# A new opening for a hybrid encoder block: 512-column value products first, conditioning rows on VectorE

## The chip, the core and the metric

The kernel runs on one NeuronCore of a Trainium2 chip. The metric is device time in microseconds (us) of one execution. In this text TensorE is PE in the profile (PEld is its weight load), VectorE is DVE, ScalarE is ACT, GpSimd is POOL, and SP is the SyncE queue that issues nearly all DMAs.

## The reference

One encoder block on a sequence of 1024 positions with 1024 features, in float32:

```
ada = silu(c) @ w_ada + b_ada            # six vectors of 1024: shift1 scale1 gate1 shift2 scale2 gate2
h = rmsnorm(x, g_mix) * (1 + scale1) + shift1
qa,ka,va,qb,kb,vb,ga,gb = split(h @ w_in)          # 6 x 512 and 2 x 1024 columns
oa = mixture_of_dilations(qa, ka, va, rel_bias)     # branch A: three banded patterns, 8 heads
ob = neighbourhood_attention_2d(qb, kb, vb, rpb)    # branch B: 2-D window, 8 heads
merged = sigmoid(ga) * (oa @ w_branch_dil) + sigmoid(gb) * (ob @ w_branch_na)
x = x + gate1 * (merged @ w_out)
h2 = rmsnorm(x, g_ffn) * (1 + scale2) + shift2
u = depthwise_conv3(h2 @ w_up)                      # 5632 columns
x = x + gate2 * ((gelu(u_gate) * u_val) @ w_down)
out = rmsnorm(x, g_final)
```

Only the opening matters here: the vector `ada`, the first norm, h, and the first products out of `w_in`.

## The kernel before, in words

**Products.** Features lie on the 128 partitions, in 8 tiles (k = 0 to 7); positions lie along the free dimension in two halves of 512. A float32 product is made of three products of rounded parts: each operand is split into a high part (`hi`, a copy in the type float32r) and a low part (`lo`, the rest), and TensorE adds hi x hi, hi x lo and lo x hi in PSUM (lines 77 to 79, and 247 to 249 for the value products). A split is one ScalarE copy (L55) and one subtraction on GpSimd or VectorE (L56).

**Conditioning.** `w_ada` comes in 12 chunks of 512 columns (2 MB each, four DMAs of two rows). VectorE multiplies each of the 8 row tiles by silu(c), one number a partition, and adds them up (`ada_rows`, L155 the first row, L157 the others); for the first four chunks ScalarE and GpSimd take some of the rows (`ada_rows_pool`, L161 and L163) and L166 joins the two sums. Four one-column matmuls with a vector of ones then add over the partitions (`ada_sums`, L141), and a VectorE op adds the bias (`piece_bias`, L263 and L265; L148 for the later chunks). The first four chunks are cut so that chunk q holds shift and scale of the feature tiles 2q and 2q + 1: h's tiles can be made two by two as the pieces come.

**h.** For a half, ScalarE squares x (L186), VectorE adds the squares (L188), TensorE adds over partitions (L91), a short chain makes 1/rms (L96 to L98), and four transposes spread it over the partitions (`pbc`, L104). x is multiplied by that (`scale_x`, L206: some tiles on VectorE, most on GpSimd); then ScalarE makes the high part of h (L212), VectorE makes h once more (L214) and subtracts (L215).

**Order.** The opening of the first half, and the norm of the second, are written out by hand for all five engines (`manual_schedule`, L288). Behind each piece of `ada` stand two feature tiles of h, their matmuls for the first q and k tiles (two products of 512 columns) and for four blocks of 128 positions of the first 256 value columns (hv = 0). Behind the hand-written part a planner with a simulated timeline orders the work: the second half of q and k, the rest of the values (256 columns at a time, st counts blocks of 128 positions, `v_product`), the copies of the values to DRAM and their rearrangement there (`va_chunks`, `vb_chunks`), the chunks 4 to 11 of `ada`, then eight rounds of attention (four of branch A, four of branch B) with the q/k products of the next round and the gate products between them. The pools of the opening are released ahead of attention, and attention's tiles (biases, values, softmax) lie where they were.

## Time and profile before

| | |
|---|---|
| runs shown | 1593.29, 1603.09, 1605.68 us (median 1603.09) |
| the profiled execution | 1599.1 us, span 1597.3 us, mean granted TensorE clock 0.98 |
| TensorE busy | 1504.6 us, 94% of the span |
| VectorE, ScalarE, GpSimd busy | 68%, 51%, 48% |
| first product of the opening starts | 27.71 us |
| attention runs on from | 199.23 us |

A timeline row reads: start, length, engine, source line, operation, the tile written and the tile read, shapes, how many were merged, and in brackets the idle time of the engine ahead of it and what ended it. Matmul lengths overlap, so the step from one to the next is read from their starts. In the busy tenths of the page each digit is one fortieth of the span, about 40 us.

### The profile page before, as it was taken

How to read it: one execution, taken by the hardware profiler on the slowest of the kernel's cores; microseconds unless marked ns; L12 is line 12 of the kernel's file. 1: busy time of each engine (PE TensorE's matmuls, PEld its weight loads, DVE VectorE, ACT ScalarE, POOL GpSimd, SP SyncE). 2: the span in 40 equal slices, each digit the busy share in tenths (PEclk: the TensorE clock that was granted, in tenths of full speed). 3: DMA queues.
4: the chain of work that ended last, by engine and by line, in shares of the span. 5: the costliest groups of instructions: out<-in, count | busy, mean ns of one | idle time of the engine just before them, and what ended most of it. 6: DMA issues, size and time to landing. Idle time of an engine off the chain costs nothing. (4 is left out here: it accounts for less than half of the span.)

```text
span 1597.3 us, 21951 instructions
## 1 busy us (share of the span) xinstructions
PE 1504.6 (94%) x7884; PEld 1283.0 (80%) x7884; DVE 1078.5 (68%) x1905; ACT 819.2 (51%) x1479; POOL 769.8 (48%) x490
## 2 busy tenths in 40 slices
PE   4898899999999999999989889999999999999998
PEld 3898888888988888888768777788888887778787
DVE  6886476666767666535542799876666667786765
ACT  4531175666766677544344544344444446475542
POOL 4452133332324444411136767676666665678621
PEclk9898999999999999999999999999999999999999
DMA  6749922222223434446544312222222223533313
GB/s 231 262 137 319 281 61 85 68 89 72 79 80 112 131 108 115 156 133 210 173 144 159 112 53 80 80 92 92 80 79 80 79 80 138 161 129 120 112 53 106
DMA packets 113525, 196.87 MB, mean 123 GB/s; under 512 B 40328, under 2 KB 61704, under 8 KB 113416
## 3 DMA queue, kind: packets, MB, share of 16 engines
q1 hardware_dynamic: 113144, 195.20, 37.3%
q8 instruction: 62, 1.02, 0.3%
q14 instruction: 47, 0.39, 0.1%
q10 hardware_dynamic: 272, 0.26, 0.1%
HBM read 158.73 MB, written 42.47 MB: 126 GB/s over the span
## 5 line engine op out<-in xcount | busy, mean ns | idle before, releaser
L56 POOL TENSOR_TENSOR wlo<-wraw,whi 128x1024 fp32r<-128x1024 f32 (+2 forms) x77 | 177.6, 2306 | 299.1 <-ACT whi L55 285.5
L77 PE MATMUL pj<-h,whi 128*128 128x512 f32 x448 | 182.2, 408 | 17.5 <-DVE kl L429 9.8
L78 PE MATMUL pj<-h,whi 128*128 128x512 f32 x448 | 180.5, 403 | 1.2 <-DVE h L215 1.2
L79 PE MATMUL pj<-h,wlo 128*128 128x512 f32 x448 | 180.4, 403 | 0.0
L56 POOL TENSOR_TENSOR wsl<-big,wsh 128x1024 fp32r<-128x1024 f32 (+1 forms) x45 | 108.9, 2422 | 49.4 <-ACT wsh L55 49.4
L1061 DVE SCALAR_TENSOR_TENSOR big<-wc,sm,big 128x256 f32<-128x256 f32 (+1 forms) x132 | 118.9, 948 | 17.3 <-ACT big L1055 17.2
L55 ACT ACTIVATE whi<-wraw 128x1024 fp32r<-128x1024 f32 (+2 forms) x81 | 81.0, 1000 | 68.9 <-PE pj L78 35.8
L77 PEld LDWEIGHTS pj<-h,whi 128*128 128x128 f32 x448 | 85.7, 192 | 35.4 <-issue 7.0
L78 PEld LDWEIGHTS pj<-h,whi 128*128 128x128 f32 x448 | 86.3, 193 | 16.9 <-DVE h L215 2.3
L79 PEld LDWEIGHTS pj<-h,wlo 128*128 128x128 f32 x448 | 86.1, 192 | 15.5
L542 ACT ACTIVATE P<-P,st 128x256 f32<-128x256 f32 x128 | 64.2, 503 | 47.7 <-DVE st L541 47.3
L541 DVE CUSTOM_DVE_ANT_0 P<-S,bias 128x256 f32<-128x256 f32 x128 | 52.2, 421 | 47.8 <-PE S L588 36.3
L474 POOL TENSOR_TENSOR vv<-vv 96x256 fp32r<-96x256 f32 (+2 forms) x32 | 40.9, 1289 | 84.3 <-ACT vv L473 53.6
L157 DVE SCALAR_TENSOR_TENSOR wada<-wada,cs 128x512 f32<-128x512 f32 x67 | 65.7, 980 | 20.4 <-DMA wada<-w_ada 18.5
L694 POOL TENSOR_SCALAR P<-P,stb 128x288 f32<-128x288 f32 (+1 forms) x32 | 40.1, 1254 | 81.4 <-DVE stb L691 63.6
L1061 DVE SCALAR_TENSOR_TENSOR big<-pj,sm,big 128x512 f32<-128x512 f32 x132 | 67.8, 563 | 16.4 <-ACT big L1055 16.4
L429 DVE SCALAR_TENSOR_TENSOR kl<-pj,ks 64x512 fp32r<-64x512 f32 x64 | 56.3, 880 | 30.6 <-ACT ks L427 30.0
L1055 ACT ACTIVATE big<-wc,sm 128x512 f32<-128x512 f32 x44 | 35.8, 815 | 76.6 <-DVE wc L878 46.1
L247 PE MATMUL pv<-vwh,h 128*128 128x256 f32 x256 | 74.0, 289 | 0.0
L249 PE MATMUL pv<-vwh,h 128*128 128x256 f32 x256 | 73.5, 287 | 0.0
L248 PE MATMUL pv<-vwl,h 128*128 128x256 f32 x256 | 73.0, 286 | 0.0
L56 POOL TENSOR_TENSOR wsl<-wraw,wsh 128x768 fp32r<-128x768 f32 (+1 forms) x23 | 49.9, 2168 | 43.3 <-ACT wsh L55 43.3
(361 smaller groups left out, 4908.6 us busy)
## 6 DMA issues: line engine op xcount, KB each, us to landing
wada<-w_ada SPq DMA_DIRECT2D x47, 512.0 KB, 5.0
wraw<-w_in SPq DMA_DIRECT2D x36, 512.0 KB, 3.8
big<-w_up SPq DMA_DIRECT2D x22, 512.0 KB, 5.5
wraw<-w_up SPq DMA_DIRECT2D x22, 512.0 KB, 3.6
as<-big SPq DMA_DIRECT2D x22, 512.0 KB, 3.0
big<-as SPq DMA_DIRECT2D x22, 512.0 KB, 6.9
wraw<-w_down SPq DMA_DIRECT2D x24, 384.0 KB, 4.1
gs<-gs SPq DMA_DIRECT2D x32, 256.0 KB, 2.0
```

The lines of the kernel that those rows point to most:

```text
L55: act.activation(hi, raw, AF.Copy)
L56: lo_eng.tensor_tensor(lo, raw, f(hi), OP.subtract)
L77: pe.matmul(psum, whi[:, k0 + k], mhi, start=k == 0, stop=False)
L78: pe.matmul(psum, whi[:, k0 + k], mlo, start=False, stop=False)
L79: pe.matmul(psum, wlo[:, k0 + k], mhi, start=False, stop=k == n - 1)
L157: dve.scalar_tensor_tensor(acc, wt[t], cs[:, t:t + 1], acc, OP.mult, OP.add)
L247: pe.matmul(p, hhi, hi[:, k], start=fresh and k == 0, stop=False, skip_group_check=True)
L248: pe.matmul(p, hhi, lo[:, k], start=False, stop=False, skip_group_check=True)
L249: pe.matmul(p, hlo, hi[:, k], start=False, stop=k == KT - 1, skip_group_check=True)
L429: dve.scalar_tensor_tensor(ll[x], pp[a], 0.125, f(kh[a]), OP.mult, OP.subtract)
L542: act.activation(pp, pp, AF.Exp, bias=mi, scale=-1.0, accum_out=li)
L1061: dve.scalar_tensor_tensor(y[:, dst], src, wt, y[:, dst], OP.mult, OP.add)
```

## The change

- **Values first.** The opening makes value products alone, 512 columns wide: the value weights come as a new input `w_v` in four loads of 512 KB a branch, and a 128 x 512 PSUM bank holds one block of 128 positions. The hand-written part now holds all four groups (branch A and B, each half): the first phase makes branch A's first half, two feature tiles behind each piece; then come B first half, A second half, B second half as 24 steps of 12 matmuls. The first q and k products come behind all that, all four of them, and the chunks 4 to 11 of `ada` stand between the steps: VectorE's rows at every second step from 4 to 18, their sums at every second step from 9 to 23. The weights for q and k are split at step 12, and `va_chunks` is issued once, at step 17.
- **Rows on VectorE.** ScalarE and GpSimd take no rows of `w_ada`. For the pieces 1 to 3 VectorE takes six rows, and TensorE adds the last two directly (`ada_sums` with silu(c) in place of ones). Whole chunks have tiles of their own.
- **Low parts a tile behind.** x is not scaled on its own any more: VectorE multiplies x by the scale and by 1/rms in one op into PSUM (`stage`), ScalarE makes the high part from it, and VectorE the low part from it, one tile later. GpSimd does only the low parts of the value weights.
- **Idle products.** `warm(n)` issues n products of the identity with itself, whose result nobody reads: 12 ahead of the norm's sums, 3 ahead of the spread of 1/rms, 8 behind it, 6 behind the first piece's sum.
- **Layout.** x comes in four loads of 512 KB a half, the input rearranged on the host for that; the place that loads x again later in the kernel follows the new layout. The pool of the q/k tiles and its PSUM banks are allocated behind the opening.

The core of the diff (`-` before, `+` after):

```diff
-    def modulate(x, hf, ks, lo_eng):
-        for k in ks:
-            a, b = am1[:, k:k + 1], ada[:, k:k + 1]
-            hi, lo = h[hf, k] = h_tile(), h_tile()
-            act.activation(hi, x[k], AF.Identity, bias=b, scale=a)
-            t = early.tile([128, 512], FT, name="mt", bufs=4)
-            dve.tensor_scalar(t, x[k], a, b, OP.mult, OP.add)
-            lo_eng[k % 2].tensor_tensor(lo, t, f(hi), OP.subtract)
+    def modulate(x, hf, ks, pb):
+        last = ()
+        for k in [*ks, None]:
+            if k is not None:
+                hi, lo = h[hf, k] = h_tile(), h_tile()
+                t, b = stage(), ada[:, k:k + 1]
+                dve.scalar_tensor_tensor(t, x[k], am1[:, k:k + 1], pb, OP.mult, OP.mult)
+                act.activation(hi, t, AF.Identity, bias=b)
+            if last:
+                dve.scalar_tensor_tensor(*last, OP.add, OP.subtract)
+            last = k is not None and (lo, t, b, f(hi))
+    def warm(n):
+        for _ in range(n):
+            pe.matmul(idle, idt, idt, start=True, stop=True)
+    def v_split(raw, w, kp):
+        for i in range(2):
+            split(raw[:, i], w[0][:, 2 * kp + i], w[1][:, 2 * kp + i], pool)
+    def v_products(w, hf, k, banks, ts=range(4)):
+        hi, lo = w
+        for t in ts:
+            p = banks[t]
+            hhi, hlo = (x[:, t * 128:t * 128 + 128] for x in h[hf, k])
+            pe.matmul(p, hhi, hi[:, k], start=k == 0, stop=False, skip_group_check=True)
+            pe.matmul(p, hhi, lo[:, k], start=False, stop=False, skip_group_check=True)
+            pe.matmul(p, hlo, hi[:, k], start=False, stop=k == KT - 1, skip_group_check=True)
...
+        idle = ps.tile([128, 512], FT, name="pj", bufs=5)[:, :128]
+        warm(12)
+        accs = squares(x[0], (dve, dve))
+        pcol = norm_sums(accs)
+        acc = ada_rows(rows[0], range(3))
+        r = rstd_of(pcol, 4)
+        warm(3)
+        pb = bcast(r, ps, "pc")
+        acc = ada_rows(rows[0], range(3, 8), acc)
+        warm(8)
+        v_split(raws[0], vw[0], 0)
+        pa = ada_sums([(acc, ones)])
+        warm(6)
+        banks = v_banks()
+        for q in range(4):
+            piece_bias(q, pa)
+            modulate(x[0], 0, range(2 * q, 2 * q + 2), pb)
+            v_products(vw[0], 0, 2 * q, banks)
             if q < 3:
+                v_split(raws[q + 1], vw[0], q + 1)
+                acc = ada_rows(rows[q + 1], range(6))
+                pa = ada_sums([(rows[q + 1][t], cs[:, t:t + 1]) for t in (6, 7)], stop=False)
             else:
+                accs = squares(x[1], (dve, dve))
+            v_products(vw[0], 0, 2 * q + 1, banks, (0, 1))
+            if q < 3:
+                ada_sums([(acc, ones)], pa)
+            v_products(vw[0], 0, 2 * q + 1, banks, (2, 3))
+        raws = [v_load(1, kp) for kp in range(4)]
+        vw.append((t16("b1"), t16("b2")))
+        rows = {4: ada_load(4, "t0"), 5: ada_load(5, None)}
+        pcol = norm_sums(accs)
+        r = rstd_of(pcol, 4)
+        for kp in range(2):
+            v_split(raws[kp], vw[1], kp)
...
+        for n in range(24):
+            g, k = divmod(n, 8)
+            br, hf = ((1, 0), (0, 1), (1, 1))[g]
+            if k == 0:
+                v_out(*old)
+                banks = v_banks()
+                old = br, hf, banks
+            if n == 17:
+                va_chunks(slice(0, 512))
+            v_products(vw[br], hf, k, banks)
+            if n == 0:
+                pb = bcast(r, ps, "pc")
+                for kp in (2, 3):
+                    v_split(raws[kp], vw[1], kp)
+                modulate(x[1], 1, range(8), pb)
+            if n in (5, 6):
+                qk_raw.append(w_load(w_in[4 * (n - 5)]))
+            i = n // 2 - 2
+            if n % 2 == 0 and 0 <= i < 8:
+                accs[i] = ada_rows(rows[4 + i], range(KT))
+                if i < 6:
+                    rows[6 + i] = ada_load(6 + i, (None, "t0")[i % 2 == 0])
+            if n % 2 and n >= 9:
+                i = (n - 9) // 2
+                ada_bias(4 * (i + 4), ada_sums([(accs[i], ones)]))
+            if n == 12:
+                qk_w = [w_split(qk_raw[i], pool) for i in range(2)]
+        v_out(*old)
...
-    qk = qk_tiles(0, 0, qk_w, qk_psum)
...
+    qk = qk_tiles(0, 0, qk_w)
...
-        "xT": x[0][_POS].T.reshape(KT, 128, S),
+        "xT": x[0][_POS].T.reshape(4, 2, 128, 2, 512).transpose(3, 0, 2, 1, 4),
```

More of the change, by code (lines that the diff above doesn't have):

```diff
@@ L217, in v_load @@
[L217 to L231 removed]
+    xpool = tc.alloc_tile_pool(name="xs", bufs=4, side="right", reuse_waits="tile")
@@ new lines, in hybrid_encoder, with t16, small_tile, stage @@
+    early = tc.alloc_tile_pool(name="early", bufs=1, reuse_waits="tile")
+    ps = tc.alloc_tile_pool(name="ps0", bufs=1, space=PSUM, reuse_waits="tile")
+    def t16(tag, dtype=FR):
+        return tpool.tile([128, KT, 512], dtype, name=tag)
+    def small_tile():
+        return early.tile([128, 512], FT, name="mt", bufs=6)
+    def stage():
+        return ps.tile([128, 512], FT, name="st", bufs=2)
+    def ada_sums(parts, pa=None, stop=True):
+        first = pa is None
+        pa = stage() if first else pa
+        for i, (w, col) in enumerate(parts):
+            for m in range(4):
+                pe.matmul(pa[:, m:m + 1], w[:, m * 128:(m + 1) * 128], col, start=first and i + m == 0,
+                          stop=stop and i == len(parts) - 1 and m == 3, skip_group_check=True)
+        return pa
@@ new lines, in ada_rows, with ada_load @@
+    def ada_rows(rows, ts, acc=None):
+        for t in ts:
+            if acc is None:
+                acc = small_tile()
+                dve.tensor_scalar(acc, rows[t], cs[:, t:t + 1], None, OP.mult)
+            else:
+                dve.scalar_tensor_tensor(acc, rows[t], cs[:, t:t + 1], acc, OP.mult, OP.add)
+        return acc
+    def ada_load(j, tag):
+        if tag:
+            tile = t16(tag, FT)
+            tiles = [tile[:, t:t + 2] for t in range(0, KT, 2)]
+        else:
+            tiles = [x_tile().rearrange("p (a b) -> p a b", a=2) for _ in range(4)]
+        for i, t in enumerate(tiles):
+            sp.dma_start(t, w_ada[j][:, 2 * i:2 * i + 2])
+        return [t[:, i] for t in tiles for i in range(2)]
@@ new lines, in ada_bias, with x_load, squares @@
+    def ada_bias(c0, pa):
+        cc = slice(c0, c0 + 4)
+        dve.tensor_tensor(ada[:, cc], pa[:, :4], b_ada[:, cc], OP.add)
+    def x_load(hf):
+        x = []
+        for kp in range(4):
+            t = x_tile() if hf == 0 else wpool.tile([128, S], FT, name=("whi", "wlo")[kp % 2])
+            sp.dma_start(t.rearrange("p (a b) -> p a b", a=2), xT[hf, kp])
+            x += [t[:, 512 * i:512 * i + 512] for i in range(2)]
+        return x
+    def squares(x, engines):
+        accs = []
+        for k in range(KT):
+            sq = small_tile()
+            act.activation(sq, x[k], AF.Square)
+            if k % 4:
+                engines[k // 4].tensor_tensor(accs[-1], accs[-1], sq, OP.add)
+            else:
+                accs.append(sq)
+        return accs
@@ L372, in qk_tiles @@
+        v_out(*old)
+    dve.scalar_tensor_tensor(am2, ada[:, 32:40], 1.0, g_ffn, OP.add, OP.mult)
+    ps.release()
+    early.release()
+    tpool.release()
+    xpool.release()
+    qkpool = tc.alloc_tile_pool(name="qk", bufs=3, reuse_waits="tile")
+    ps_g = tc.alloc_tile_pool(name="psg", bufs=2, space=PSUM, reuse_waits="tile")
+    def qk_tiles(br, pr, ws=None):
         qt, kt = ((0, 4), (12, 16))[br]
```

282 lines of the change are left out of this document (53 added, 229 removed).

## The prediction

> **What bounds the kernel now.** I read the page first, then the busy time by stage, then TensorE's timeline up to the first attention.
>
> ```profile
> span 1597.3 us, 21951 instructions
> PE 1504.6 (94%) x7884; PEld 1283.0 (80%) x7884; DVE 1078.5 (68%) x1905; ACT 819.2 (51%) x1479; POOL 769.8 (48%) x490
> PE   4898899999999999999989889999999999999998
> ```
> ```profile
> 0.00:27.70 27.70, 8.58 (x36) 7.84 (x36) 16.15 (x23) 13.60 (x22) 9.31 (x10) 1.00 0.85 306
> 52.70:64.90 12.20, 9.06 (x41) 7.61 (x42) 8.52 (x13) 3.41 (x5) 2.50 (x2) 0.72 1.01 378
> 75.20:124.40 49.20, 49.09 (x369) 46.66 (x368) 40.02 (x51) 17.69 (x32) 23.07 (x18) 1.00 0.44 145
> 131.60:199.20 67.60, 62.83 (x465) 60.48 (x465) 37.27 (x53) 11.57 (x22) 11.06 (x6) 0.95 0.92 297
> 199.20:400.00 200.80, 199.22 (x1157) 173.53 (x1158) 133.10 (x397) 136.05 (x330) 67.44 (x48) 0.98 0.25 75
> ```
>
> The columns of the second fence are stage, length, busy PE, PEld, DVE, ACT and POOL, granted clock, DMA share, GB/s. TensorE bounds the kernel (94%). Behind 199.2 us, where attention starts, it is busy 199.22 of 200.8 us, so time that the opening saves should reach the end almost whole. The opening's loss sits ahead of 75 us.
>
> ```profile
> 13.18 1.87 PE L91 MATMUL pcol<-ones,sq 128*128 128x1 f32 x8 [0.93 <-DVE sq L188]
> 15.76 1.12 PE L104 MATMUL pbc<-idt,rs 128*128 128x128 f32 x4 [0.70 <-DVE rs L98]
> 27.71 0.80 PE L77 MATMUL pj<-h,whi 128*128 128x512 f32 x1 [3.83 <-ACT h L212]
> ...
> 54.91 0.57 PE L77 MATMUL pj<-h,whi 128*128 128x512 f32 x1 [2.83 <-ACT h L212]
> 56.41 0.79 PE L78 MATMUL pj<-h,whi 128*128 128x512 f32 x1 [0.93 <-DVE h L215]
> 57.01 0.63 PE L79 MATMUL pj<-h,wlo 128*128 128x512 f32 x1
> ...
> 60.84 0.63 PE L79 MATMUL pj<-h,wlo 128*128 128x512 f32 x1
> ...
> 69.57 0.28 PE L247 MATMUL pv<-vwh,h 128*128 128x256 f32 x1
> ...
> 75.15 0.28 PE L249 MATMUL pv<-vwh,h 128*128 128x256 f32 x1
> ...
> 103.19 0.95 PE L141 MATMUL pada<-ones,wada 128*128 128x1 f32 x8
> 104.00 0.36 PE L249 MATMUL pv<-vwh,h 128*128 128x256 f32 x1
> ...
> 131.56 1.84 PE L141 MATMUL pada<-ones,wada 128*128 128x1 f32 x8 [7.19 <-issue]
> 143.91 0.95 PE L141 MATMUL pada<-ones,wada 128*128 128x1 f32 x8
> ...
> 182.35 0.39 PE L77 MATMUL pj<-h,whi 128*128 128x512 f32 x1
> ...
> 192.44 0.40 PE L79 MATMUL pj<-h,wlo 128*128 128x512 f32 x1
> 192.67 0.95 PE L141 MATMUL pada<-ones,wada 128*128 128x1 f32 x8
> 199.23 0.58 PE L557 MATMUL S<-ks,qs 128*128 128x256 f32 x1 [4.80 <-DVE st L541]
> ```
>
> From starts: 48 matmuls of 256 columns lie between 69.57 and 75.15, 0.119 us each; 45 of 512 columns between 182.35 and 192.44, 0.229 us each; after the gap of 54.91, 10 of them between 57.01 and 60.84, 0.426 us each: half rate. One vector sum (L141, "x8") takes 0.81 us (103.19 to 104.00).
>
> **The change, part by part. Matmuls.** Before: 768 value matmuls x 0.119 = 91.4 us. After: 2 branches x 2 halves x 4 tiles x 8 k x 3 = 384 x 0.229 = 87.9: 3.5 us less. The four q/k products (96 x 0.229 = 22 us) only move behind the opening. In the first phase equal work is done: before 96 value matmuls of 256 (11.4 us) and 48 q/k matmuls (11.0), ended at 75.3; after 96 value matmuls of 512 (22.0). I call that end A.
>
> **Up to the first product.** The rows for VectorE, GpSimd, ScalarE and DMA:
>
> ```profile
> 10.85 2.28 DVE L188 TENSOR_TENSOR sq<-sq,mt 128x512 f32<-128x512 f32 x3 [0.51 <-ACT mt L186]
> 16.11 4.19 DVE L157 SCALAR_TENSOR_TENSOR wada<-wada,cs 128x512 f32<-128x512 f32 x3
> ...
> 40.42 0.16 DVE L263 TENSOR_TENSOR ada<-pada,sm 128x4 f32<-128x4 f32 x1 [1.98 <-PE pada L141]
> 52.74 0.15 DVE L263 TENSOR_TENSOR ada<-pada,sm 128x4 f32<-128x4 f32 x1
> 64.93 0.17 DVE L263 TENSOR_TENSOR ada<-pada,sm 128x4 f32<-128x4 f32 x1 [3.17 <-PE pada L141]
> 81.15 2.48 DVE L206 TENSOR_TENSOR h<-h,pbc 128x512 f32<-128x512 f32 x4 [1.62 <-ACT mt L201]
> ```
> ```profile
> L155 DVE TENSOR_SCALAR wada<-wada,cs x12: 456/484/2533, 15.6 to 178.6; 128x512 f32<-128x512 f32 x12
> ...
> L157 DVE SCALAR_TENSOR_TENSOR wada<-wada,cs x67: 743/752/2870, 16.1 to 187.4; 128x512 f32<-128x512 f32 x67
> ```
> ```profile
> 16.79 1.28 POOL L163 TENSOR_TENSOR kl<-kl 128x512 f32<-128x512 f32 x1 [16.37 <-ACT kl L161]
> 43.47 1.49 POOL L56 TENSOR_TENSOR wlo<-wraw,whi 128x512 fp32r<-128x512 f32 x1 [2.56 <-ACT whi L55]
> 81.20 4.04 POOL L206 TENSOR_TENSOR h<-h,mt 128x512 f32<-128x512 f32 x3 [2.50 <-ACT mt L201]
> ```
> ```profile
> 41.03 1.52 ACT L212 ACTIVATE h<-h,ada,am 128x512 fp32r<-128x512 f32 x2 [8.38 <-DVE am L265]
> ```
> ```profile
> GB/s 0 75 290 239 239 335 339 413 401 426 393 371 412 418 401 259 98 350 265 0 0 0 19 287 44 0 177 335 288 254 393 289 25 68 352 376 231 392 430 391
> wada<-w_ada SPq DMA_DIRECT2D x47, 512.0 KB, 5.0
> ```
>
> The second fence is the two groups of row steps: duration min/median/max in ns. A row step (L157) takes 0.75 us, the multiply that opens a chunk (L155) 0.5; beside GpSimd (16.11 against 16.79) it took 1.40. L206, which has one operand in PSUM, took 0.62 beside GpSimd (81.15 against 81.20). The new modulate ops read one operand from PSUM and write PSUM or SBUF. No row writes PSUM from VectorE; I bound such an op by 0.62 and 1.40 and take 0.65, from L206, the nearest.
>
> Squares end at 13.1 (10.85 + 2.28). The new 512 KB loads of x may bring them forward: in slices of 1.5 us the rate is 240 to 290 GB/s while x comes in 256 KB pieces and about 400 with w_ada's 512 KB pieces; I take 1 us. From 12.1: the multiply and two row steps 2.0, rstd 0.7 (the gap of 15.76), five row steps 3.75, twice 0.65 more beside the split on GpSimd: 19.9; the sum, cold like 13.18's, 1.9: the first piece's bias op starts at **22**. Bias and scale 0.6 (40.42 to 41.03), one modulate op 0.65 and one ScalarE op 0.76 (41.03) bring the first product to 24, against 27.71. Of the 29 idle products the last six stand between the sum and the first product: 2.2 us of room, six 128-column products like 15.76's four (0.28 each) 1.7, so nothing; double that if each takes two passes, 1.2 late.
>
> **The loop over pieces.** Before, the bias ops started at 40.42, 52.74 and 64.93: 12.2 us a piece. After, from a bias op: bias 0.6, one modulate op and ScalarE's tile 1.4, and the low part, queued behind the second modulate op, 0.65: 2.7. Then TensorE: 12 matmuls 2.75, rows 6 and 7 as sums 1.6, six matmuls 1.4, the sum 0.8, semaphore 0.2: 9.4. VectorE meanwhile: bias 0.6, four ops 2.6 and a wait 0.3, the multiply 0.5, five row steps 3.75 and up to 2 x 0.65 beside GpSimd: 9.0, then sum and semaphore: 10.0. I take 9.5, and 11 for the first, which starts at half rate (eight matmuls x 0.2 = 1.6). Pieces: 22, 33, 42.5, 52. DMA covers it: x, four pieces of w_ada and the value weights are 12.1 MB, 30 us at 400 GB/s and some 34 with the start, and all but the last piece have tiles of their own (it waits for the first one's, free at 20). A is then 52 + 2.7 + 24 x 0.229 = **60**, against 75.3: **15 us**.
>
> **From A to attention.** Before: 199.2 - 75.3 = 123.9 us with 672 value matmuls 80.0, 48 q/k 11.0, 48 of the next q 11.0, eight sums 6.5, norm 2.4 = 110.9; lost 13.0, of which 7.19 and 4.80 are the two gaps. After: 288 x 0.229 = 66.0, q/k 22.0, next q 11.0, sums 6.5, norm 2.4 = 107.9. New losses: the second half's norm stands ahead of the splits on ScalarE, so branch 1's first weights are split only after TensorE's sums, rstd 0.7, a split at most 0.76 (as L212) and a low part 1.28 to 1.49 (16.79, 43.47): TensorE waits about 2.5 behind its norm sums, and another 1 until the value banks, whose copies (0.76 at most) stand behind those splits, are out. At the end the q product waits for the last copies: 0.5. The attention gap I leave at 2, between 0 (bias and values load while q and k are made) and the 4.80 of now. Sum 6. Gain 13.0 - 6 + 3.0 = **10 us**. The remaining edits (x layout, later q/k pool, reload of x) move no bytes of the rest; I cost them at nothing, covered by a TensorE that is busy 99% there; uncovered, one 0.5 us issue.
>
> VectorE's row steps for the eight later chunks are 0.5 + 7 x 0.75 = 5.8 us a chunk, against 2 x 12 x 0.229 + 0.8 = 6.3 on TensorE: hidden, if data come.
>
> **Sum:** 15 + 10 = 25; for planning behind the opening I take 1 off: **24 us**. The profiled execution took 1599.1 us (span 1597.3 and 1.8 around it); the runs shown are 1593.3 to 1605.7, median 1603.1. From the middle of the profiled time and the median, 1601: **1577 us**.
>
> **The clock rule.** The trace has half rate after an idle stretch of 2.83 and 0.93 us. In my loop the wait between the last matmuls of one piece and the next low part is 0.2 + 2.7 - 1.4 = 1.5 us, so I run it at full rate; were it twice that, the rows would have it at half rate, 24 x 0.2 = 4.8 us a piece. The Trainium skill, "TensorE: Matmul & The Clock Gate", Part 1, says the clock falls after a window of about 3.4 us without work and rises after as long a busy one; by it a wait of 3 us would leave the forecast as it is, where the row of 54.91 makes it 1591.
>
> **Rivals.** *Cold loop* (0.12): gaps add up (a modulate op at 1.40, a late w_ada piece) and TensorE runs at 0.72 as in 52.7 to 64.9: three pieces x 4.8 = 14 us, gain 10, 1591. For it: it does so today. Against: less work on GpSimd, no op in front of modulate.
>
> *Slower: sums in a fixed order* (0.08): the eight later sums now stand in TensorE's written order between value products. Today a chunk takes (192.67 - 143.91) / 4 = 12.2 us, as VectorE waits for w_ada. Counted from the last piece (52), step 0 ends at 16 (A, 8.4; norm, splits and copies, 5; a step, 2.75), and the eighth chunk's sum is due before step 23's end, 22 x 2.75 + 7 x 0.8 later: 82. VectorE starts the chunks at 16 + 8 x 1.5 of modulating = 28, so the eighth is ready at 28 + 8c: delay 8c - 54. It eats the gain from c = 9.8; at 12.2 it is 43.6: 1601 - 24 + 44 = 1621. Behind a late load stand, on SP's queue, the value results on their way out, whose tiles the row steps share. For it: 5.0 us to landing, and a reload that starts only when the tile is read. Against: two whole chunks of tiles instead of one, and no gathers on SP's queue until step 17.
>
> *Attention starts no earlier* (0.10): the planner puts all 4.80 and a cold stretch behind q/k, and shuffles later fillers; 8 to 12 lost: gain 12 to 16, 1587. Nothing in the trace shows the new order, so I cannot exclude it.
>
> *The idle products do nothing* (inside the forecast): they end before the work does, at 1.6 us: 1579.
>
> **Numbers.** Forecast (gain 16 to 34, 1567 to 1585) 0.64: the bounds are A at 56 to 65 (modulate ops and row steps at 0.62 or 1.40, first product late or not) and losses of 4 to 10 behind it. More than that 0.06; the rivals 0.30. About 16 us, 1%, is what a measurement can tell from no change. Faster: 0.64 + 0.06 = 0.70; within: 0.12 + 0.10 = 0.22; slower 0.08. The range leaves out the slower rival and half of the largest gains, and holds the 4 us between profiled time and median: 1560 to 1597.
>
> **What would show it.** First product near 24; pieces at 33, 42.5, 52 by the bias op; matmul starts 0.229 apart through the loop; A at 60; second-half value products gap of 2 to 3; later sums without idle ahead of them; first attention product running from about 172. Wrong if pieces stay 12 apart, if sums wait for DMA, or if the gain to 199 is missing from the span.

## The result, and the profile after

| | before | changed |
|---|---|---|
| median (range), 9 runs each | 1598.93 us (1593.29 to 1605.68) | 1591.39 us (1585.06 to 1596.18) |
| profiled execution, its span | 1599.1, 1597.3 us | 1590.6, 1588.7 us |
| ratio, 95% interval | | 0.9947, 0.9928 to 0.9966 |

The change gains 7.5 us, half of one per cent. The forecast was 1577 us, a gain of 24, with 1560 to 1597 as its range: the time lies in the range, the gain is a third of the one forecast.

The page of the changed kernel, its head:

```profile
span 1588.7 us, 21184 instructions
PE 1513.5 (95%) x7582; PEld 1273.0 (80%) x7582; DVE 1058.9 (67%) x1905; ACT 804.8 (51%) x1451; POOL 741.8 (47%) x475
```

Busy time by stage in the changed kernel; the columns are as in the prediction's second fence:

```profile
22.50:61.10 38.60, 35.17 (x168) 27.53 (x169) 33.17 (x44) 12.05 (x21) 8.14 (x6) 0.91 0.82 316
61.10:70.10 9.00, 7.13 (x32) 5.40 (x31) 0.34 (x2) 6.30 (x13) 6.10 (x5) 0.81 0.62 245
70.10:132.00 61.90, 61.90 (x300) 52.10 (x299) 50.34 (x70) 12.41 (x18) 9.58 (x6) 1.00 0.67 235
132.00:148.20 16.20, 11.45 (x45) 9.27 (x44) 11.31 (x20) 2.33 (x4) 0.00 (x0) 0.79 0.87 352
...
390.00:446.00 56.00, 49.87 (x304) 44.73 (x303) 40.69 (x110) 38.65 (x85) 12.92 (x9) 0.91 0.23 66
```

The second phase runs without a gap (61.90 of 61.90 us), and two stages stand out: 132 to 148 us, where 16.2 us hold 11.45 us of TensorE at a clock of 0.79, and 390 to 446 us, far behind the opening, with 49.87 of 56 us at 0.91.

TensorE's timeline in the opening of the changed kernel (start, length, idle ahead and what ended it):

```profile
22.52 0.50 PE L236 MATMUL pj<-a,h 128*128 128x512 f32 x1 [0.52 <-ACT h L202]
...
30.30 1.05 PE L140 MATMUL st<-ones,mt 128*128 128x1 f32 x8 [1.24 <-DVE mt L151]
...
40.98 1.05 PE L140 MATMUL st<-ones,mt 128*128 128x1 f32 x8 [0.34 <-DVE mt L151]
...
51.67 1.05 PE L140 MATMUL st<-ones,mt 128*128 128x1 f32 x8 [1.13 <-DVE mt L151]
...
63.98 0.49 PE L236 MATMUL pj<-b,h 128*128 128x512 f32 x1 [1.01 <-ACT b L55]
...
137.78 1.47 PE L140 MATMUL st<-ones,mt 128*128 128x1 f32 x8 [4.75 <-DVE ada L167]
```

First product at 22.5, sums of the pieces 10.7 us apart, first phase over at 61.1 against 75.3 before: 14 us gained. Then a sum of the later chunks waits 4.75 us, and what follows it runs at half rate to 144.8.

To see where the gain goes, I count for each kernel the matmuls that are still to run, each at the step it has at full rate (0.229 us for 512 columns), and compare when the two kernels have the same amount left. That is the **lead**: how many us earlier a kernel reaches the point that the kernel before reaches at the time given.

| lead at (time of before) | 114 | 144 | 165 | 215 | 396 | 465 | 653 | 1272 |
|---|---|---|---|---|---|---|---|---|
| changed kernel | 9.8 | 20.4 | 12.5 | 18.7 | 16.3 | 7.6 | 8.7 | 7.2 |

The lead rises where the kernel before waits (7.19 us ahead of 131.56, 4.80 ahead of 199.23) and falls twice in the changed one: by 8 us at the late sum, and by 8.7 between 396 and 465, in the fourth round of attention. The two losses together are about what the forecast is off.

### The profile page after: what moved, and what is told of

It reads as the page before. It is cut to its first block, busy times and chain, and to the rows that moved or that the text cites. A ratio compares the mean times of both kernels' runs of the same rounds, so it can differ in the third digit from the quotient of the medians.

```text
span 1588.7 us, 21184 instructions
## 1 busy us (share of the span) xinstructions
PE 1513.5 (95%) x7582; PEld 1273.0 (80%) x7582; DVE 1058.9 (67%) x1905; ACT 804.8 (51%) x1451; POOL 741.8 (47%) x475
## 4 chain that ended last, share of the span: by engine, by line
PE 63%; DVE 14%; DMA 6%; ACT 6%; POOL 5%; issue 5%; SPq 1%; DVEq 0%; ACTq 0%; POOLq 0%
PE pj L817 9%; PE pj L816 9%; PE pj L818 9%; PE pj L77 8%; PE pj L79 8%; PE pj L78 8%; DVE mt L151 2%; DMA g<-gs 2%; DVE big L1012 2%; PE pj L378 2%; ACT ks L403 2%; DMA wraw<-w_down 2%; PE O L666 1%; POOL wlo L56 1%; DVE kl L405 1%
## 5 line engine op out<-in xcount | busy, mean ns | idle before, releaser
L56 POOL TENSOR_TENSOR wlo<-wraw,whi 128x1024 fp32r<-128x1024 f32 (+1 forms) x77 | 179.8, 2336 | 289.9 <-ACT whi L55 277.9
L77 PE MATMUL pj<-h,whi 128*128 128x512 f32 x448 | 179.9, 402 | 8.9 <-DVE kl L405 7.0
L78 PE MATMUL pj<-h,whi 128*128 128x512 f32 x448 | 178.4, 398 | 0.0
L1012 DVE SCALAR_TENSOR_TENSOR big<-wc,sm,big 128x256 f32<-128x256 f32 (+1 forms) x132 | 117.0, 934 | 17.3 <-ACT big L1006 17.2
L55 ACT ACTIVATE whi<-wraw 128x1024 fp32r<-128x1024 f32 (+1 forms) x79 | 80.7, 1021 | 83.3 <-POOL wc L957 20.3
L79 PEld LDWEIGHTS pj<-h,wlo 128*128 128x128 f32 x448 | 84.8, 189 | 15.7
L385 POOL TENSOR_SCALAR qb<-qs 128x256 fp32r<-128x256 f32 x32 | 26.4, 851 | 105.9 <-DVE qs L369 51.1
L403 ACT ACTIVATE ks<-pj 64x512 fp32r<-64x512 f32 x64 | 53.7, 838 | 21.1 <-DVE kl L405 10.0
L1038 ACT ACTIVATE big<-big 128x1024 f32<-128x1024 f32 x22 | 23.3, 1060 | 79.7 <-DVE big L1012 79.7
L55 ACT ACTIVATE wsh<-big 128x1024 fp32r<-128x1024 f32 (+1 forms) x45 | 44.8, 999 | 36.4 <-POOL big L781 21.9
```

The lines of the kernel that those rows point to most:

```text
L55: act.activation(hi, raw, AF.Copy)
L56: lo_eng.tensor_tensor(lo, raw, f(hi), OP.subtract)
L77: pe.matmul(psum, whi[:, k0 + k], mhi, start=k == 0, stop=False)
L78: pe.matmul(psum, whi[:, k0 + k], mlo, start=False, stop=False)
L79: pe.matmul(psum, wlo[:, k0 + k], mhi, start=False, stop=k == n - 1)
L403: act.activation(kh[x], pp[a], AF.Copy, scale=0.125)
```

## The experiments

Each ratio is to the kernel before, run on the same chip; its medians lay between 1598.96 and 1600.23 us.

| run | median us | ratio, 95% interval |
|---|---|---|
| e1 gathers on ScalarE's queue | 1595.91 | 0.9979, 0.9962 to 0.9995 |
| e11 gathers on GpSimd's queue | 1591.95 | 0.9951, 0.9933 to 0.9968 |
| e9 gathers behind the last value result | 1585.84 | 0.9912, 0.9894 to 0.9929 |
| e13 late gathers | 1584.55 | 0.9902, 0.9880 to 0.9923 |
| e16 list 2,2,1,3 | 1582.04 | 0.9886, 0.9871 to 0.9901 |
| e14 late gathers, list 2,1,2,3 | 1580.11 | 0.9886, 0.9869 to 0.9903 |
| e15 late gathers, list 2,2,1,3 | 1577.32 | 0.9865, 0.9846 to 0.9883 |
| e10 list 2,2,2,1,2 | 1596.51 | 0.9981, 0.9967 to 0.9995 |
| e2 no idle products | 1592.20 | 0.9958, 0.9942 to 0.9973 |
| e5 weights split first | 1593.22 | 0.9971, 0.9956 to 0.9987 |
| e6 rows shared | 1592.97 | 0.9962, 0.9947 to 0.9978 |
| e7 low parts at once | 1608.65 | 1.0056, 1.0030 to 1.0082 |
| b1 before, gathers on ScalarE's queue | 1599.20 | 1.0006, 0.9991 to 1.0021 |
| b2 before, list 2,2,1,3 | 1601.94 | 1.0014, 1.0001 to 1.0028 |
| b4 before, late gathers | 1599.02 | 0.9990, 0.9976 to 1.0004 |
| b3 before, late gathers, list 2,2,1,3 | 1592.91 | 0.9962, 0.9952 to 0.9972 |

### Why does the sum at 137.8 wait?

Theory: the gathers of branch B's values (L450, `vb_chunks`) stand on SyncE's queue ahead of a reload of `w_ada`. Rival: the reload is late for bandwidth or for its tile. SyncE's queue and VectorE in the changed kernel:

```profile
114.85 11.35 SPq L450 DMA_DIRECT2D vb<-vbc  x14
126.30 2.17 SPq L162 DMA_DIRECT2D t<-w_ada  x4
```
```profile
112.20 5.48 DVE L151 SCALAR_TENSOR_TENSOR mt<-t,cs,mt 128x512 f32<-128x512 f32 x7
...
131.56 0.49 DVE L149 TENSOR_SCALAR mt<-t,cs 128x512 f32<-128x512 f32 x1 [7.63 <-DMA t<-w_ada]
```

The rows that free the tile end at 117.6; the reload is issued at 126.3, behind 14 gathers that take 11.35 us to issue; VectorE waits 7.63 us for it.

**e1: the gathers on ScalarE's queue.**

```diff
-                sp.dma_start(vb_s[cb]...[r, :, :, cc], ...)
+                act.dma_start(vb_s[cb]...[r, :, :, cc], ...)
```

> The rearrangement of branch B's values in DRAM (32 DMAs, L450) is issued from ScalarE's queue instead of SP's; nothing else is edited. In the changed kernel the planner put 14 of them on SP's queue between the reloads of w_ada for the last chunks: the load for the seventh later chunk was issued at 126.3 us though its tile was free at 117.6, and TensorE stood 4.75 us in front of a sum at 137.8 and then ran 14 matmuls at half rate. Theory (queue order): the load is issued near 118, the gap of 4.75 and the half rate behind it go, the last sum of the opening comes at about 140 instead of 147.4. Rival (bandwidth): the rearrangement still runs at that time and the data come late all the same; the sum stays near 147. Theory for the end: the 7.5 us reach the end, 1584, and 1576 if the new plan of the attention stage also loses the 8 us that were lost between 390 and 445 us. Rival (attention cannot use an earlier start): the end stays at 1591.

The three sums behind the old gap start at 134.49, 140.85 and 147.21 with no idle time ahead of them. That alone does not tell the queue from bandwidth, as TensorE came late to them by more than was saved. ScalarE issues the gathers now, and the copies that empty the value banks stand behind them:

```profile
111.28 15.84 ACTq L450 DMA_DIRECT2D vb<-vbc  x15
```
```profile
127.88 0.80 PE L236 MATMUL pj<-b,h 128*128 128x512 f32 x1 [12.11 <-ACT mt L246]
```

TensorE waits 12.11 us for a bank; the lead at 165 is 6.4. Nor is the reload issued near 118, as expected, but at 124.91. SyncE's queue holds no gathers now, yet what SyncE waited for ahead of the reload is, by the profile, the landing of gathers (total us, times, longest):

```profile
SPq L162 <- DMA vb<-vbc: 11.4, 2, 10.8
```

**e11: on GpSimd's queue** (`pool.dma_start` in the same place).

> The same 32 gathers, issued on GpSimd's queue and left to the planner's place. Theory (order in SyncE's queue): the w_ada reloads are no longer behind them and the 4.75 us ahead of the sum at 137.8 go, as with ScalarE's queue; GpSimd then makes the low parts of the next weights later, by up to 16 x 0.6 = 10 us, and if TensorE needs them in that time the wait takes the place of the one removed. Rival (bandwidth): the gap stays. Time between 5 us below and 3 us above the changed kernel.

This run tells the two apart. GpSimd issues the first 16 gathers at 107.5 to 120.3, about when SyncE did in the changed kernel, and the reload goes out as soon as its tile is read (its last row step ends at 118.26):

```profile
118.29 1.79 SPq L162 DMA_DIRECT2D t<-w_ada  x4
```

So the order in the queue it was. The gap shrinks to 1.39 us, which go back to a load of the chunk before (VectorE waits 2.56 us for it at 122.68), and the lead at 165 is 18.7. The other 16 gathers are issued at 153 to 167 among GpSimd's own work, and a gap stands ahead of the score products:

```profile
168.85 1.38 DVE L405 SCALAR_TENSOR_TENSOR kl<-pj,ks 64x512 fp32r<-64x512 f32 x2 [4.34 <-ACT ks L403]
```
```profile
170.75 0.58 PE L507 MATMUL S<-ks,qs 128*128 128x256 f32 x1 [5.39 <-DVE st L491]
```

It is not GpSimd that came last there: its first addition of the bias had ended at 164.8, and VectorE's softmax (170.26) stood behind a low part that waited 4.34 us for ScalarE. The planner's order is another one from the first attention products on, so this loss is not shown to be the gathers' on GpSimd. The lead is 9.6 at 185 and 14.1 at 215, and the median is that of the changed kernel.

**e9: on SyncE, in the order written by hand, behind the last value result.**

```diff
+        for hv in range(2):
+            vb_chunks(slice(hv * 256, hv * 256 + 256))      # last lines of the hand-written part
...
-            if n == 0:
-                for hv in range(2):
-                    vb_chunks(slice(hv * 256, hv * 256 + 256))
```

> The 32 gathers of branch B's values are issued on SyncE's queue behind the last value result instead of between the w_ada reloads. Theory (the reload of chunk 5 stood 12 us behind gathers in one queue): its multiply no longer waits 7.63 us, the sum at 137.8 has no 4.75 us ahead of it and the products behind it run at full rate, so the opening gains some 7 us up to the q/k products. Rival (the loads were late for bandwidth or for their tiles): the gap stays at 3 to 5 us. What may take its place: 32 issues of about 0.6 us, 19 us in all, now stand on SyncE ahead of the dilated biases, so the first attention products may start up to 19 us minus the 22 us of q/k products later, which is 0 to 5 us. If the rest of the kernel keeps its order, the time is 4 to 7 us below the changed kernel's 1590.6 in the profile; if the planner's order of fillers behind it moves as well, anything within 6 us of that.

The reload is issued at 118.17, no sum waits, and the lead at 165 is 20.3 where the changed kernel has 12.5. As the expectation feared, the 32 gathers now delay attention's first loads:

```profile
142.50 25.99 SPq L260 DMA_DIRECT2D vb<-vbc  x32
...
169.16 0.43 SPq L481 DMA_DIRECT2D bias<-p_bias  x1
```

They took 26 us to issue, not the 19 that I had reckoned, and attention gives back 2 us by 215 (18.1). The median is 5.6 below the changed kernel's.

**e13: late gathers.** Four small copies out of the first round's result, into rows that the gathers overwrite, make the gathers wait for that round. Leaving them at a later place in the program would not do: the planner issues them as soon as branch B's values are there.

```diff
             if n == 0:
+                for cb in range(4):
+                    sp.dma_start(vb_s[cb][0:4], o_scr[0][0][0:4, 0:512])
                 for hv in range(2):
                     vb_chunks(slice(hv * 256, hv * 256 + 256))
```

> The 32 gathers of branch B's values stay on SyncE's queue but can start only when the first attention round has written its result (four 8 KB copies from that result into the rows that the gathers then overwrite make them wait), so they are out of the opening and out of the way of the first attention loads. The order of TensorE's instructions is that of the changed kernel to the end of attention. Theory (both losses are named rightly): the sums' gap of 4.75 us and its half rate go, as with the gathers behind the last value result, but without that kernel's late biases: lead on the kernel before 19 to 21 us at the first attention products (the changed kernel: 16) and 18 to 21 through the first three rounds; the fourth round loses its 6 to 8 us as before, since the order there is the same: the end is 11 to 14 us below the kernel before. Rival (attention waits for something else in the first rounds, so that an earlier start is given back there): lead 16 again by 230 us, and the end as the changed kernel's, 8 to 9 us below.

```profile
117.96 1.76 SPq L162 DMA_DIRECT2D t<-w_ada  x4
```

The reload is issued at 117.96, as soon as the tile is read (its last row step ends at 117.9). The lead is 20.5 at 165, 23.8 at 215 and 20.3 at 396, close to the 25 of the forecast; then it falls to 12.6 at 465 as foretold, and the end is 6.8 us below the changed kernel.

**b1: the kernel before with its gathers on ScalarE's queue** (the same one-word edit).

> The kernel before with the same edit as the first: the rearrangement on ScalarE's queue. Control for what a new plan alone does. In its opening no gap stood behind these DMAs (the gap of 7.19 us at 131.6 lies ahead of the first of them, at 146.8), so the theory expects attention to run on from 199 within 2 us and the end within 3 us of the kernel before; a shift of 5 us or more would show that a new plan alone moves the attention stage by as much as the changed kernel lost there.

Lead within 0.3 us of nothing up to 653, and no difference in the median. The gap of 4.80 us ahead of the first score products stays, though no gather stands on SyncE's queue: ahead of attention's first load, issued at 189.42 (189.69 in the kernel before), SyncE waits for the landing of gathers instead.

```profile
SPq L738 <- DMA vb<-vbc: 3.8, 1, 3.8
```

### Why does the fourth round lose 8 us?

The waits of TensorE from 360 to 480 us (engine, tile and line that waited <- what it waited for: total us, times, longest). The changed kernel:

```profile
PE S L507 <- DVE st L491: 4.3, 2, 2.4
PE pj L77 <- DVE kl L405: 0.8, 1, 0.8
PE O L521 <- ACT th L496: 0.7, 1, 0.7
```

The score products (S) wait twice for VectorE's softmax to free a bank, and behind each of the two waits the clock falls to half rate (at 394.2 for 3.4 us, at 438.6 for 6.8 us):

```profile
393.79 0.38 PE L507 MATMUL S<-ks,qs 128*128 128x256 f32 x1 [1.94 <-DVE st L491]
...
438.08 0.39 PE L507 MATMUL S<-ks,qs 128*128 128x256 f32 x1 [2.41 <-DVE st L491]
```
```profile
440.00:445.00 5.00, 5.00 (x17) 4.20 (x17) 4.78 (x14) 2.07 (x6) 2.27 (x3) 0.50 0.14 52
```

In the kernel before, over the same 120 us, these are the waits, and the clock from 385 to 485 us is 1.00:

```profile
PE pj L77 <- DVE kl L429: 1.9, 2, 1.2
PE S L557 <- DVE st L541: 1.1, 1, 1.1
```

Theory: it is the order that the planner makes, in which the products between the score products stand elsewhere. Rival: VectorE's softmax bounds attention, so a TensorE that comes early must wait there, and the lead is bound to go. The list `counts` says how many gate tiles (11 us of products each) the program names behind each of the eight rounds.

**e10: the list (2,2,2,1,2,1,0,6) for (2,2,2,2,1,1,0,6).**

> The number of gate tiles listed behind the eight attention rounds is (2,2,2,1,2,1,0,6) for (2,2,2,2,1,1,0,6): one gate tile is moved behind the first round of neighbourhood attention; the opening is the same. Theory (the 8 us that the changed kernel loses against the one before in the fourth dilated round, 390 to 446 us, come of the planner's order of fillers in that stage, not of the chip): the idle rows of 394 to 445 and the half rate of 439.6 to 445.1 change with the order, and the kernel's lead on the one before, 16 us ahead of that stage, is another behind it (5 us or more away from 8, to either side). Rival (attention there is bound by VectorE's softmax whenever TensorE is early, so that the lead must be given back): the lead falls to 7 to 9 us again, whatever the fillers' place.

It tells little on the question, by my own mistake: TensorE's order stays that of the changed kernel up to the end of that round (lead 7.7 at 465). Behind it the lead falls to -3.2 at 512 and is 5.0 at 653: a list alone can cost 4 us.

**e7** (below) tells more: it reaches 396 with a lead of 1.5 us and still falls to -7.2 at 465. A kernel that is not early loses the same 8.7 us, so the rival falls.

**e16: the list (2,2,1,3,1,1,0,6)**, one gate tile moved from behind the third round to behind the fourth.

```diff
-        counts = (2, 2, 2, 2, 1, 1, 0, 6)
+        counts = (2, 2, 1, 3, 1, 1, 0, 6)
```

> The changed kernel with the gate tiles listed (2,2,1,3,1,1,0,6) and the gathers where its planner had put them. Theory (two losses that add: gathers 7 us of which 4 reached the end, products missing in the fourth round 6 to 7 us): the gap of the sums stays (4.75 us), the fourth round's gaps go; the end is 4 to 7 us below the changed kernel, 12 to 16 below the one before. Rival (the list of gate tiles helps only with the late gathers, as they leave SyncE's queue free for the weights of the products): within 2 us of the changed kernel.

The sum's gap stays and the lead is the changed kernel's up to 396 (16.5). It is 11.2 at 465, and 15.5 and 15.7 at 512 and 653: of the 7.6 us that the changed kernel loses from 396 to 653, 0.8 are left. The end is 9.4 us below the changed kernel.

**e15 and e14: late gathers with (2,2,1,3) and with (2,1,2,3).**

> As the one before with (2,2,1,3): the product is taken out of the third round alone, where the order keeps 23 us of products beside 16 us of attention work (from 40 to 56 us of attention work), less than in any other stretch. Theory (shortage of products): the fourth round's gaps go, but 3 to 8 us of new gaps stand in the third; the end within 4 us of the late gathers alone. Rival (the fourth round's gaps have a cause of their own there, a late load of its biases or keys): they stay whatever products are beside.

> As the one before, and the gate tiles listed behind the first rounds are (2,1,2,3) for (2,2,2,2), so that one product of 11 us is taken out of the second and third round and lies in the fourth, where the changed kernel's order has 31 us of products beside 16 us of attention work on TensorE, and this one 39. Theory (the fourth round's 6 to 8 us are a shortage of products to run while VectorE works on the softmax): the gaps of that round (1.94, 0.79, 2.41, 0.67 us and the cold stretch) go, and the end is 5 to 8 us below the kernel with the late gathers alone, if the second and third round, with 11 us less to run, still have enough. Rival (VectorE's softmax bounds all of attention, so what one round is given another lacks): the same gaps appear in the second or third round, and the end is within 2 us of the late gathers alone.

e15's waits from 360 to 480 us:

```profile
PE pj L77 <- DVE kl L405: 1.4, 2, 0.8
PE T L602 <- ACT whi L55: 1.4, 1, 1.4
PE T L602 <- DVE u L604: 1.1, 1, 1.1
PE S L507 <- DVE st L491: 0.6, 1, 0.6
```

The two long waits for the softmax are down from 4.3 to 0.6 us; other, shorter ones came. From 396 to 653 e15's lead goes from 18.8 to 18.0 (e13: 20.3 to 12.3), and its median, 1577.32, is 14.1 below the changed kernel: the fastest here. e14 loses in the second and third rounds first (lead 22.4 at 283, 10.3 at 396) and has 18.4 at 653, 4.4 us better than e13 at the end. But the reason I gave is not borne out. If the number of products beside were what counts, e15 should lose more: between 48 and 76 us of attention's own TensorE work, e13 runs some 63 us of products, e14 68 and e15 57. What is left is where they stand, and which property of the order decides I leave open.

### Are the two losses the change's own?

**b2: the kernel before with the list (2,2,1,3,1,1,0,6).**

> The kernel before with the gate tiles listed (2,2,1,3,1,1,0,6). Theory (the fourth round's loss belongs to the order that the planner makes for the changed kernel; the one before lost nothing there: gaps of 0.19 and 1.10 us): no gain, within 3 us of the kernel before or slower by up to 6. Rival (this list is simply better for both, and the change has nothing to do with it): 4 to 8 us below the kernel before, as with the changed one.

It gains nothing (1.7 us slower): the list mends the changed kernel's order and not this one's.

**b3: the kernel before with late gathers and that list.**

> The kernel before with both mends, late gathers and the list (2,2,1,3,1,1,0,6). Theory: its gathers lie singly between other loads from 147 us on, behind most of its w_ada reloads, so that moving them gives 0 to 3 us; with the list the end is within 4 us of the kernel before, and the changed kernel with both mends, 1577.3, keeps 18 to 22 us on it, which is what the opening is worth. Rival (both mends would serve any opening): 8 to 13 us below the kernel before, and the opening is worth only 9 to 14.

7.3 us faster, less than its rival's 8 and more than its theory's 4. The lead is 8.7 at 215 and 8.8 at 653. Its first score products have no gap ahead of them, nor have those of b4 below, which moves the gathers alone. So the 4.80 us, and the half rate behind them, came with the gathers in the kernel before too. Their place on SyncE's queue ahead of the biases does not explain it, as b1 has the gap without it. Ahead of the first softmax (198.74) GpSimd's addition of the bias ends last, and in the kernel before it stands behind a weight split:

```profile
183.89 5.75 SPq L481 DMA_DIRECT2D vb<-vbc  x7
```
```profile
195.42 2.34 POOL L56 TENSOR_TENSOR wlo<-wraw,whi 128x1024 fp32r<-128x1024 f32 x1 [43.84 <-ACT whi L55]
197.72 1.95 POOL L531 TENSOR_TENSOR bias<-bias,lnm 128x384 f32<-128x384 f32 x2
```

In b3 and b4 the planner puts that addition ahead of the split (at 185.24 and 188.86). Whether the earlier bias loads or the new order on GpSimd removes the gap, these runs do not separate.

**b4: late gathers alone in the kernel before.**

> The kernel before with the late gathers alone. Theory (gathers stood on SyncE's queue ahead of the first attention's biases in that kernel too, and its gap of 4.80 us and the half rate behind it were theirs; the list is no help to it): the lead on the kernel before is 8 to 9 us from 216 us on, as with both mends, and stays through attention: the end is 6 to 9 us below the kernel before, within 2 us of both mends together (1592.9). Rival (the 7.3 us of both mends come of the two together): within 3 us of the kernel before.

The lead at 215 is 5.3 us, not 8 to 9, and then the same thing happens as in the changed kernel: from 396 to 465 it falls from 4.7 to -3.8. Its waits from 360 to 480 us:

```profile
PE S L557 <- DVE st L541: 4.3, 2, 2.4
PE pj L77 <- DVE kl L429: 0.8, 1, 0.8
PE O L571 <- ACT th L546: 0.7, 1, 0.7
```

These are the changed kernel's waits to the tenth, in a kernel with the old opening: the loss is no property of the opening. Over the stage, from 382 to 455 us of the changed kernel, TensorE's order in b4 is that of the changed kernel matmul for matmul, and so it is in e9, though attention was led up to differently in each. The kernel before has another order there, and so has e11, which loses 3.4 us from 396 to 465 with the same list. The gains, against the kernel before of the same chip:

| us | gathers as planned | late gathers |
|---|---|---|
| before, list 2,2,2,2 | 0 | 0.2 |
| before, list 2,2,1,3 | -1.7 | 7.3 |
| changed, list 2,2,2,2 | 7.5 | 14.6 |
| changed, list 2,2,1,3 | 18.2 | 21.9 |

The new opening alone is worth 7.5, 14.4 (14.6 - 0.2), 19.9 (18.2 + 1.7) or 14.6 us (21.9 - 7.3), by what stands behind it. With neither of the two losses on either side it is 14.6, and the first phase alone gave 14. A spread of 12 us by order alone says how far any one of these differences can be trusted.

### What the parts of the change are worth

**e2: no idle products** (the four `warm` calls taken out).

> The changed kernel without its 29 idle products. Theory: the first twelve value products run at half rate (12 x 0.2 = 2.4 us late) and the norm's sums too (0.8), so the first phase ends near 63 instead of 61.1, and the end is 0 to 3 us later. Rival (they do nothing): every time within 1 us up to 61. Rival (they cost): the six in front of the first product go, and it starts up to 1 us earlier.

The pieces' sums come at 32.36, 42.95 and 53.64, 2.0 us later, and the first phase ends at 62.6, near the 63 of the theory; the lead at 114 is 8.6 against 9.8. At the end 0.8 us, inside the intervals: not told apart.

**e5: branch B's first weights split ahead of the second half's squares.**

```diff
+                raws = [v_load(1, kp) for kp in range(4)]      # ahead of squares(x[1], ...)
+                vw.append((t16("b1"), t16("b2")))
+                for kp in range(2):
+                    v_split(raws[kp], vw[1], kp)
                 accs = squares(x[1], (dve, dve))
```

> The first two splits of branch B's value weights stand ahead of the second half's squares instead of behind its norm. Theory: the two gaps of 1.0 and 0.9 us in front of step 0 and its half rate go, and step 0 ends near 67.5 instead of 70; the norm comes 2.6 us later on ScalarE, which nobody waits for, as modulate ended at 82 and its first user came at 92. Whether the 2.5 us reach the opening's end depends on the sums: if they wait for w_ada's late reload, the last sum stays at 147 and the end at 1591; if they do not, 145 and 1589.

The wait for the weights is replaced by one for the squares, as the norm's sums stand ahead of the products on TensorE:

```profile
62.73 1.05 PE L89 MATMUL pc<-ones,mt 128*128 128x1 f32 x8 [2.03 <-DVE mt L183]
```

The lead at 114 is 7.7, 2 us worse.

**e6: rows 0 to 2 of the pieces 1 to 3 on ScalarE and GpSimd again.**

```diff
-                acc = ada_rows(rows[q + 1], range(6))
+                for t in range(3):
+                    act.activation(rows[q + 1][t], rows[q + 1][t], AF.Copy, scale=cs[:, t:t + 1])
+                for t in (1, 2):
+                    pool.tensor_tensor(rows[q + 1][0], rows[q + 1][0], rows[q + 1][t], OP.add)
+                acc = ada_rows(rows[q + 1], range(3, 6))
+                dve.tensor_tensor(acc, acc, rows[q + 1][0], OP.add)
```

> The changed kernel with the row sums of pieces 1 to 3 shared as in the kernel before: rows 0 to 2 scaled on ScalarE and added on GpSimd, rows 3 to 5 and the join on VectorE. Theory (VectorE's chain of modulate and five row steps, about 9 us, makes the 10.7 us of a piece): 1.5 to 2.5 us less VectorE work a piece, pieces 8.5 to 10 us apart, first phase ended at 56 to 60 instead of 61.1. Rival (GpSimd beside VectorE stretches VectorE's operations, 0.75 to 1.40, and the sum's way through TensorE to the bias sets the pace): pieces 10.5 to 12 us apart, 61 to 65. Behind the first phase the lead changes by the same amount, and the end by 0 to 4 us.

Sums at 30.56, 41.65 and 52.74, 11.1 us apart against 10.7: VectorE has fewer rows and waits for GpSimd's sum instead.

```profile
47.48 3.34 DVE L151 SCALAR_TENSOR_TENSOR mt<-t,cs,mt 128x512 f32<-128x512 f32 x2
51.99 0.69 DVE L298 TENSOR_TENSOR mt<-mt,t 128x512 f32<-128x512 f32 x1 [1.16 <-POOL t L296]
```

Two row steps took 3.34 us beside GpSimd's additions, where five take 4.80 in the changed kernel. The median is 1.6 us above it, inside the intervals: rows on VectorE cost nothing, and hardly gain.

**e7: each low part directly behind its tile.**

```diff
-            if last:
-                dve.scalar_tensor_tensor(*last, OP.add, OP.subtract)
-            last = k is not None and (lo, t, b, f(hi))
+            dve.scalar_tensor_tensor(lo, t, b, f(hi), OP.add, OP.subtract)
```

> Low parts directly behind their tile instead of one tile behind; all else as in the changed kernel. Theory (in the first phase a piece is 10.7 us because VectorE's chain of modulate, rows and join ends last): VectorE waits for ScalarE's tile twice in a piece, 0.8 to 1 us each, so the pieces stand 11.5 to 12.5 us apart and the first phase ends at 64 to 66 us instead of 61.1; modulating a half (8 tiles) costs 5 us more of VectorE behind 61 too, of which TensorE shows 0 to 4. In all 3 to 8 us later at the end of the opening. Rival (TensorE's own work and the sum's way to the bias set the pace): less than 1 us in the first phase.

Sums at 31.99, 44.19 and 56.37, 12.2 us apart: the pace of the kernel before. In the second half every low part waits for ScalarE, at 2.17 us a tile:

```profile
75.57 0.76 DVE L199 SCALAR_TENSOR_TENSOR st<-whi,am,pbc 128x512 f32<-128x512 f32 x1 [6.76 <-PE pbc L102]
77.09 0.75 DVE L201 SCALAR_TENSOR_TENSOR h<-st,ada,h 128x512 fp32r<-128x512 f32 x1 [0.76 <-ACT h L200]
77.75 0.75 DVE L199 SCALAR_TENSOR_TENSOR st<-whi,am,pbc 128x512 f32<-128x512 f32 x1
```

The lead is 4.6 at 114 and 4.8 at 215, the end 17.3 us above the changed kernel. The expectation (3 to 8 us) was too small: VectorE begins the rows of chunk 4 at 92.95 us instead of 82.12, 5.7 us of it from the second half's tiles, which take 1.45 us each in the changed kernel. Without the tile's delay the whole change would be a loss of half a per cent.

## Why the prediction was right and wrong

**Up to the first product: right.** 24 forecast, 22.5 measured.

**The loop: right in kind, its size off.** Forecast bias ops at 22, 33, 42.5 and 52; measured 20.6, 31.4, 42.1 and 52.8, so 10.7 us a piece and not 9.5. One piece on VectorE in the changed kernel:

```profile
42.07 0.16 DVE L215 TENSOR_TENSOR ada<-st,sm 128x4 f32<-128x4 f32 x1 [1.15 <-PE st L140]
...
42.47 1.42 DVE L201 SCALAR_TENSOR_TENSOR st<-x,am,pbc 128x512 f32<-128x512 f32 x2
43.98 1.41 DVE L204 SCALAR_TENSOR_TENSOR h<-st,ada,h 128x512 fp32r<-128x512 f32 x2
45.31 1.48 DVE L149 TENSOR_SCALAR mt<-t,cs 128x512 f32<-128x512 f32 x1
46.82 4.80 DVE L151 SCALAR_TENSOR_TENSOR mt<-t,cs,mt 128x512 f32<-128x512 f32 x5
52.76 0.16 DVE L215 TENSOR_TENSOR ada<-st,sm 128x4 f32<-128x4 f32 x1 [1.15 <-PE st L140]
```

The prediction had VectorE's side at 10.0 and took 9.5, nearer to TensorE's 9.4; VectorE ends last. The mis-sized term is the multiply, put at 0.5: beside GpSimd's low parts it took 1.48. The modulate ops, bounded by 0.62 and 1.40, took 0.75. A came at 61.1 for 60, as the first piece started earlier.

**Behind A: right in size, not in its parts.** 3.5 us of waits were forecast for the weights and the banks; TensorE's step 0 and the spread of 1/rms end at 70.1, about 3.9 later than their work. The waits are 1.01 and 0.86 us (63.98 and 65.33); the other 2 us are half rate behind them, for which the forecast had no term.

**"Hidden, if data come": the first step that failed.** The rows take 5.9 us a chunk (5.8 forecast), except for one chunk that takes 10.0 beside GpSimd's split of the q and k weights. But the data did not come, and the ground given against the slower rival, no gathers on SP's queue until step 17, was wrong. The order written by hand fixes how its own instructions follow one another; the planner put others between them, gathers that the program names behind the first attention round. One reload behind 14 of them cost about 8 us of lead, and e13, which moves the gathers, ends 6.8 us lower. The slower rival, "sums in a fixed order", named this wait and its price, 8c - 54, for chunks that all come late; one chunk was.

**"For planning behind the opening I take 1 off": the second step that failed**, and with it the reading that 199 to 400 us at 99% busy means that time saved reaches the end. The stage that took 8.7 us back lies at 396 to 465 us of the kernel before, and I had read only up to 400. The rival "attention starts no earlier" had the size (8 to 12 us lost, 1587) and the planner as its cause, but the wrong place: at 215 the changed kernel was still 18.7 us ahead.

**The attention gap, put at 2 for 4.80: a gain with another cause.** It lies in the forecast's 10 us as a benefit of the change. In the changed kernel the first score products (164.81) wait for nothing. But b4, with the old opening, loses the gap too and has 5.3 us of lead at 215, by moving the gathers alone (b3, with the list as well, 8.7).

The two failed steps are some 16 us; the gain is 16.5 short of the forecast. The time is 14.4 above it, as the forecast started from 1601 and the kernel before has 1598.9. With both mended (e15) the gain is 21.9 for the 24 forecast, of which 14.6 are the opening's and the rest the gathers' and the order's: that it comes so near to 24 is luck in part.

**The clock rule.** The loop ran at full rate but for two stretches. Behind a gap of 1.24 us (30.30) and one of 1.13 (51.67) the rows are at half rate, from 32.4 and 52.8 on; behind 0.34 and 0.45 us (40.98 and 44.00) they are not. A stage of the changed kernel:

```profile
52.50:56.30 3.80, 3.80 (x12) 2.99 (x12) 3.15 (x6) 2.35 (x5) 0.00 (x0) 0.55 0.93 312
```

But the length of the gap alone does not decide it. In e2 the sums at 42.95 and 53.64 stand behind gaps of 1.12 and 1.14 us, and the clock stays at 1.00:

```profile
32.00:62.00 30.00, 26.20 (x135) 20.10 (x134) 24.91 (x35) 10.28 (x18) 5.44 (x4) 1.00 0.69 260
```

So a gap shorter than the 1.5 us that I had let pass can be enough, and need not be; what else decides stays open. It costs little: some eight matmuls, 1.6 us each time, not the 4.8 of a whole piece. The Trainium skill, "TensorE: Matmul & The Clock Gate", Part 1, has the clock fall after a window of about 3.4 us without work; the gaps of 1.24 and 1.13 us are a third of that, and the measurement decides. Its other figure, that it rises again after a busy window of the same length, agrees with the 3.8 us of the stage above, of which 3.4 are at half rate.

## What to carry to other kernels

An opening's gain is safe only up to the next place where a planner or a queue chooses an order: read which instructions can come between hand-ordered ones on each queue, above all DMAs whose data is not needed until much later, and tie those to something late. Behind it, look at every stage up to the end, not only the next one, since an automatic order that shifts can take back as much as the edit gives (8 us here, in kernels with either opening); before a change is judged by its time, give both kernels the same two or three orders. A subtraction that waits for another engine's copy belongs one tile behind it: that one line was worth 17 us here.

## What the runs showed of the hardware

- A DMA that ScalarE or GpSimd issues takes its place among that engine's own work. Fifteen gathers held ScalarE's queue for 15.84 us (e1), and TensorE waited 12.11 us for the copies behind them; on GpSimd seven took 3.71 us (e11).
- Issuing the strided gathers took 11.35 us for 14 and 25.99 us for 32, 0.81 us each, on SyncE, though a single issue row of them is 0.52 to 0.63 us long. Part of it is waiting: from 105 to 130 us of the changed kernel the profile names 4.9 us of waits of the gathers for other loads.
- One VectorE operation on 128x512 that takes 0.48 us alone took 1.48 while GpSimd worked on tiles of the same size; one that reads or writes PSUM took 0.75.
- TensorE fell to half rate after gaps of 1.13 and 1.24 us, and not after 0.45; but in e2 it did not after 1.12 and 1.14. In the changed kernel's record of the granted clock each stretch of half rate between 30 and 1500 us is 3.4 or 6.8 us long.
